# Seven half-size products in place of eight in the up projections of a fp32 MLP

## The chip, the cores and the metric

The kernel runs on one core of one Trainium2 chip. The metric is device time in microseconds of one execution, as the median of several. Its engines are called as the profile calls them: PE (matrix products), DVE (vectors), ACT (activations and copies), POOL (GpSimd), and SP, which here issues DMAs.

## The reference

The program is a block of two layers on 512 latent and 256 context tokens with D = 1024 and D_FF = 4096. Each layer runs four token mixers and then an MLP; what is changed is the MLP of layer 0, which works on all 768 tokens (layer 1 needs the latent ones only):

```python
def sq_relu_mlp(h, w1, b1, w2, b2):
    a = jax.nn.relu(h @ w1 + b1)
    return (a * a) @ w2 + b2
# in layer 0, for the latent stream and in the same way for the context
h2 = rmsnorm(x, ln2_g[l]) * (1.0 + sc2) + sh2
x = x + g2 * sq_relu_mlp(h2, mlp_w1[l], mlp_b1[l], mlp_w2[l], mlp_b2[l])
```

## The kernel before, in words

Activations lie with features on the 128 partitions and tokens along the row, latent tokens in 0 to 511, context tokens in 512 to 767. h2 is eight tiles k of 128 features, w1 has 32 columns f of 128, w2 has 32 k tiles and eight row tiles m.

Every fp32 product is made of three fp32r matmuls. An operand is split into a high part H (a cast) and a low part L (the rest), and H x bH, H x bL, L x bH are added in PSUM. `low` (L189) makes a split: the cast on ACT (L193), the subtraction through `tt` (L177) on POOL for weights and on DVE for activations. `load` (L309) brings a 256 KB weight block by one SP DMA (L315) into one of four `raw` buffers and splits it. `proj` (L323) runs the matmuls of one output tile through `mm` (L208, its matmul is L215): for weights (H, L) of four k tiles, first the 512 latent columns, then the 256 context columns.

`mlp` (L1740) works in eight chunks of four columns. `up(c)` makes four columns of h2 @ w1, each with 24 matmuls of 512 and 24 of 256 columns; `evac` applies bias and relu on ACT into `mr`, POOL squares into `mq`, and the split gives `y` and `aL`. `down(c)` runs, for each m, the four k tiles of the chunk against w2 and adds the result times g2 to x through `residual` (L1713), two DVE operations (L180) of 512 and 256 columns. The order is up(0), up(1), down(0), up(2), down(1) and so on:

```python
prev = None
for c in range(8):
    a = yield from up(c)
    if prev is not None:
        yield from down(c - 1, prev)
    prev = a
tail.append(down_last(prev))
```

The last down products, `down_last`, stand in `tail` and run inside the next layer's first stage, whose names begin with wa; at m = 1 and m = 6 it starts further work of the next layer (`near_end`). An accumulation of `down` takes one of two PSUM tiles of two banks (`p2`); there are two smaller ones as well (`p1`).

PE's order is written out by hand: `mm` chains each matmul behind the one before it, and a planner (`run`, `pipe`, `fill_step`) takes steps from the generators. At every seventh step of the MLP (`PACE["mlp"]`), and where a generator asks to wait, it fills in a step of other work, here the next layer's modulation (`mods`, tiles mod__m, lines L217 and L227); `drain` at the end of the layer runs what is left of it. The order on the other engines, SP's among them, is made by the language's scheduler.

## Time and profile before

| | us |
|---|---|
| median of 3 runs | 3298.92 (3297.35 to 3302.91) |
| the profiled execution | 3299.71 |
| its span in the trace | 3297.9 |
| PE busy | 3087.1 (94%) |
| DVE busy | 1391.9 (42%) |
| ACT busy | 1129.2 (34%) |
| POOL busy | 1373.4 (42%) |

The profile is of one execution. Busy shares are means over the whole program; a stage is read from windows of the trace. The up and down products of the changed MLP lie between about 1358 and 1878 us of the span, and its last down products behind that. A row's "idle before" names what ended the wait of that engine. "L215" is a line of the kernel before.

### The profile page before, as it was taken

How to read it: one execution, taken by the hardware profiler on the slowest of the kernel's cores; microseconds unless marked ns; L12 is line 12 of the kernel's file. 1: busy time of each engine (PE TensorE's matmuls, PEld its weight loads, DVE VectorE, ACT ScalarE, POOL GpSimd, SP SyncE). 2: the span in 40 equal slices, each digit the busy share in tenths (PEclk: the TensorE clock that was granted, in tenths of full speed). 3: DMA queues.
4: the chain of work that ended last, by engine and by line, in shares of the span. 5: the costliest groups of instructions: out<-in, count | busy, mean ns of one | idle time of the engine just before them, and what ended most of it. 6: DMA issues, size and time to landing. Idle time of an engine off the chain costs nothing. (4 is left out here: it accounts for less than half of the span.)

```text
span 3297.9 us, 48613 instructions
## 1 busy us (share of the span) xinstructions
PE 3087.1 (94%) x18344; PEld 2615.3 (79%) x18344; DVE 1391.9 (42%) x2920; ACT 1129.2 (34%) x2133; POOL 1373.4 (42%) x1126
## 2 busy tenths in 40 slices
PE   7888989899999999999999987889999999999999
PEld 5777778788888888888888876777877788788887
DVE  6644522554444454511221276444354444442223
ACT  5434423334332122422222254333333432243333
POOL 4422232323344453443333355224333455555553
PEclk9999999999999999999999988999999999999999
DMA  7343343333243456222222334444333343823332
GB/s 270 105 117 100 123 144 97 90 100 114 74 144 95 137 172 199 64 77 75 74 74 74 94 100 118 138 131 118 104 108 102 106 143 110 271 78 99 96 96 80
DMA packets 556922, 380.24 MB, mean 115 GB/s; under 512 B 45177, under 2 KB 503870, under 8 KB 556688
## 3 DMA queue, kind: packets, MB, share of 16 engines
q1 hardware_dynamic: 556056, 376.98, 38.0%
q8 instruction: 145, 2.38, 0.3%
q14 instruction: 89, 0.73, 0.1%
q10 hardware_dynamic: 632, 0.16, 0.0%
HBM read 307.52 MB, written 63.75 MB: 113 GB/s over the span
## 5 line engine op out<-in xcount | busy, mean ns | idle before, releaser
L177 POOL TENSOR_TENSOR mlp__wL<-mlp__raw,mlp__wH 128x512 fp32r<-128x512 f32 x268 | 351.6, 1314 | 455.0 <-ACT mlp__wH L193 321.4
L193 ACT CAST mlp__wH<-mlp__raw 128x512 fp32r<-128x512 f32 x268 | 166.1, 621 | 499.9 <-PE mlp__p L215 350.2
L177 POOL TENSOR_TENSOR gt__wL<-gt__raw,gt__wH 128x512 fp32r<-128x512 f32 x128 | 169.2, 1328 | 277.6 <-ACT gt__wH L193 231.2
L215 PE MATMUL mlp__p<-out__hL,mlp__wH 128*128 128x512 f32 (+1 forms) x760 | 257.1, 353 | 3.8 <-DVE out__hL L517 2.0
L215 PE MATMUL mlp__p<-out__hH,mlp__wH 128*128 128x512 f32 (+1 forms) x760 | 259.8, 353 | 0.5 <-ACT out__hH L516 0.5
L180 DVE SCALAR_TENSOR_TENSOR mlp__x<-mlp__p,modT,mlp__x 128x512 f32<-128x512 f32 (+1 forms) x169 | 106.4, 657 | 335.4 <-PE mlp__p L215 329.2
L215 PE MATMUL mlp__p<-mlp__y,mlp__wH 128*128 128x512 f32 (+1 forms) x672 | 231.9, 356 | 0.0
L215 PE MATMUL mlp__p<-mlp__aL,mlp__wH 128*128 128x512 f32 (+1 forms) x672 | 231.2, 355 | 0.0
L177 DVE TENSOR_TENSOR mlp__aL<-mlp__mq,mlp__y 128x768 fp32r<-128x768 f32 (+1 forms) x64 | 85.7, 1339 | 302.4 <-ACT mlp__y L193 302.2
L215 PE MATMUL gt__m<-mod__hH,gt__wH 128*128 128x512 f32 (+1 forms) x512 | 172.4, 353 | 8.1 <-DVE spec__filt L177 3.2
L215 PE MATMUL mlp__p<-out__hH,mlp__wL 128*128 128x512 f32 (+1 forms) x760 | 177.6, 351 | 0.0
L215 PE MATMUL gt__m<-mod__hL,gt__wH 128*128 128x512 f32 (+1 forms) x512 | 167.3, 343 | 0.0
L215 PEld LDWEIGHTS mlp__p<-out__hL,mlp__wH 128*128 128x128 f32 x760 | 143.5, 190 | 24.8 <-DVE out__hL L517 3.2
L177 POOL TENSOR_TENSOR ml__wL<-ml__raw,ml__wH 128x512 fp32r<-128x512 f32 x64 | 84.0, 1312 | 190.1 <-ACT ml__wH L193 171.8
L215 PEld LDWEIGHTS mlp__p<-out__hH,mlp__wH 128*128 128x128 f32 x760 | 144.3, 190 | 22.0 <-issue 2.2
L215 PE MATMUL mlp__p<-mlp__y,mlp__wL 128*128 128x512 f32 (+1 forms) x672 | 155.8, 354 | 0.0
L215 PEld LDWEIGHTS mlp__p<-out__hH,mlp__wL 128*128 128x128 f32 x760 | 130.3, 190 | 18.8
L215 PEld LDWEIGHTS mlp__p<-mlp__y,mlp__wH 128*128 128x128 f32 x672 | 126.8, 189 | 19.9 <-issue 2.2
L215 PEld LDWEIGHTS mlp__p<-mlp__aL,mlp__wH 128*128 128x128 f32 x672 | 127.1, 189 | 18.0
L193 ACT CAST gt__wH<-gt__raw 128x512 fp32r<-128x512 f32 x128 | 79.1, 619 | 177.4 <-DMA gt__raw<-in_w_in_dram 114.4
L215 PEld LDWEIGHTS mlp__p<-mlp__y,mlp__wL 128*128 128x128 f32 x672 | 115.0, 189 | 17.6
L215 PEld LDWEIGHTS gt__m<-mod__hH,gt__wH 128*128 128x128 f32 x512 | 98.5, 192 | 21.4 <-DVE spec__filt L177 5.2
(574 smaller groups left out, 7948.4 us busy)
## 6 DMA issues: line engine op xcount, KB each, us to landing
mlp__raw<-in_mlp_w_dram SPq DMA_DIRECT2D x240, 256.0 KB
mod__raw<-in_w_mod_dram SPq DMA_DIRECT2D x160, 256.0 KB
gt__raw<-in_w_in_dram SPq DMA_DIRECT2D x128, 256.0 KB
ml__raw<-in_w_in_dram SPq DMA_DIRECT2D x64, 256.0 KB
hy__raw<-in_w_in_dram SPq DMA_DIRECT2D x48, 256.0 KB
spec<-spec__kk SPq DMA_DIRECT2D x80, 128.0 KB
ga__raw<-in_w_in_dram SPq DMA_DIRECT2D x32, 256.0 KB
hy__spec<-spec SPq DMA_DIRECT2D x16, 512.0 KB
```

The source lines that it names most:

```text
L177: (eng or nc.vector).tensor_tensor(o, a, b, op)
L180: nc.vector.scalar_tensor_tensor(o, a, s, b, op0, op1)
L193: nc.scalar.copy(H, src)
L215: in_order(nc.tensor.matmul(ps, lhsT=a, rhs=b, start=start, stop=stop_), cost)
```

## The change

In layer 0 alone (`fast`) the MLP works in 16 chunks of two columns. Columns 0 to 3 are made as before. The other 28 go by pairs: `pair(f)` treats columns f and f + 1, times the two halves of the k tiles, as a 2 x 2 block matrix of weights, and h2, k halves by token halves of 384, as the other one, and forms their product by the seven-product scheme of Strassen in Winograd's order of additions. A product is 12 matmuls of 384 columns on four k tiles.

- `combos()` makes the sums of activation blocks once: for each of four k, the operations on DVE that are marked tr, ts, tt and t3, and three splits. It is a generator that stands in the pipe beside the MLP (`later`). `into_b12` splits the last of them into hH and hL in place.
- `pair` loads four blocks of w1, forms four combinations of weights on DVE (ws, w1r, raw, raw), and splits seven blocks, where the two columns had four. The products' results are put together by one ACT copy and seven DVE additions of 384 columns, six of them into `wu` and `mr`, and relu runs on those.
- The square is formed in place (`squared`).
- `weights2` loads two row tiles m of w2 in one block; `down` runs two k tiles for each m, 16 chunks of eight accumulations, with twice as many calls of `residual`.
- `mod_units(..., ahead=False)` changes the order of the modulation steps' loads.

The core of the diff (left out are the parts of `proj` that put `nk` for 4, and unchanged surroundings):

```diff
+
+        fast = len(segs) > 1
+        step = 2 if fast else 4
+        last_c = 32 // step - 1
+        half = w.stop // 2
+        lo_, hi_ = slice(0, half), slice(half, 2 * half)
+        T = {}
+        early = []
+
+        def combos():
+
+            while not all(p in hdone for p in pieces):
+                yield 0.3
+            whole = lambda k: (hH[:, k, w].bitcast(F32), hL[:, k, w].bitcast(F32))
+            homes = [yslot(), yslot(), yslot(), yslot(), big(F32R, "tc"), big(F32R, "tc"), big(F32R, "tc"), big(F32R, "tc")]
+            homes += [sp.tile([P, TOT], F32R, tag="g", name=uid("tc"), bufs=4) for _ in range(3)] + [slot(F32R, "tc")]
+            hold = [slot(name="t3") for _ in range(2)]
+            for k in range(4):
+                r, s, t = slot(name="tr"), slot(name="ts"), slot(name="tt")
+                tt(r[:, w], *whole(k), ALU.add)
+                tt(s[:, w], *whole(4 + k), ALU.add)
+                tt(t[:, lo_], r[:, hi_], r[:, lo_], ALU.subtract)
+                yield 1.5
+                tt(t[:, hi_], s[:, hi_], t[:, lo_], ALU.subtract)
+                T[3, k] = hold[k // 2][:, hi_ if k % 2 else lo_]
+                tt(T[3, k], s[:, hi_], r[:, hi_], ALU.subtract)
+                H, L = homes[2 * k], homes[2 * k + 1]
+                low(H[:, w], L[:, w], t[:, w])
+                T[1, k], T[2, k] = (H[:, lo_], L[:, lo_]), (H[:, hi_], L[:, hi_])
+                yield 1.5
+                tt(s[:, lo_], s[:, lo_], t[:, hi_], ALU.subtract)
+                H, L = (homes[8 + 2 * (k // 2) + x][:, hi_ if k % 2 else lo_] for x in range(2))
+                low(H, L, s[:, lo_])
+                T[4, k] = H, L
+                yield 4.0
+            T["all"] = True
+
+        def into_b12():
+
+            for k in range(4):
+                low(hH[:, k, hi_], hL[:, k, hi_], T[3, k])
+
+        def b(i, j):
+            return lambda k: (hH[:, 4 * i + k, hi_ if j else lo_], hL[:, 4 * i + k, hi_ if j else lo_])
+
+        def product(ps, W, mov_):
+            H, L = W
+            for k in range(4):
+                bH, bL = mov_(k)
+                mm(ps, H[:, k, :], bH, k == 0, False)
+                mm(ps, H[:, k, :], bL, False, False)
+            for k in range(4):
+                mm(ps, L[:, k, :], mov_(k)[0], False, k == 3)
+            yield 0.0
+
+        def pair(f):
+
+            while "all" not in T:
+                yield 0.3
+            if f == 4:
+                into_b12()
+            A = {}
+            view = lambda t: t.rearrange("p (k n) -> p k n", k=4)
+            for i, x in ((0, 0), (1, 0), (1, 1), (0, 1)):
+                A[i, x] = slot(name="w1r")[:, :512] if i else rawtile()
+                src = I["mlp_w1"][l][:, (f + i) * P : (f + i + 1) * P]
+                newest[0] = nc.sync.dma_start(view(A[i, x]), wcols(src, x).rearrange("(k p) n -> p k n", p=P))
+            s1 = slot(name="ws")[:, :512]
+
+            def split(t):
+                H, L = whalf()
+                low(H, L, view(t), leng=nc.gpsimd)
+                return H, L
+
+            W11 = split(A[0, 0])
+            tt(s1, A[1, 0], A[1, 1], ALU.add)
+            tt(A[1, 0], A[0, 0], A[1, 0], ALU.subtract)
+            tt(A[0, 0], s1, A[0, 0], ALU.subtract)
+            W2 = split(A[0, 0])
+            W12 = split(A[0, 1])
+            tt(A[0, 1], A[0, 1], A[0, 0], ALU.subtract)
+            W3 = split(A[1, 0])
+            pp_ = p2()
+            pa, pc_ = pp_[:, 0:half], pp_[:, 512 : 512 + half]
+            pb_, pd = p1()[:, :half], p1()[:, :half]
+            x_, u_, r0, r1 = (slot(name=n) for n in ("wx", "wu", "mr", "mr"))
+            bias = [vcol(vt, "mlp_b1", f + i) for i in range(2)]
+            relu = lambda d, s, i: act(d, s, AF.Relu, bias=bias[i])
+            yield from product(pa, W11, b(0, 0))
+            nc.scalar.copy(x_[:, lo_], pa)
+            W1 = split(s1)
+            yield from product(pb_, W2, lambda k: T[2, k])
+            tt(x_[:, hi_], pb_, x_[:, lo_], ALU.add)
+            W22 = split(A[1, 1])
+            yield from product(pc_, W12, b(1, 0))
+            tt(r0[:, lo_], pc_, x_[:, lo_], ALU.add)
+            relu(r0[:, lo_], r0[:, lo_], 0)
+            W4 = split(A[0, 1])
+            yield from product(pd, W3, b(0, 1))
+            tt(u_[:, lo_], pd, x_[:, hi_], ALU.add)
+            yield from product(pa, W1, lambda k: T[1, k])
+            tt(u_[:, hi_], pa, x_[:, hi_], ALU.add)
+            tt(r1[:, hi_], pa, u_[:, lo_], ALU.add)
+            yield from product(pb_, W22, lambda k: T[4, k])
+            tt(r1[:, lo_], pb_, u_[:, lo_], ALU.add)
+            relu(r1[:, w], r1[:, w], 1)
+            yield from product(pc_, W4, b(1, 1))
+            tt(r0[:, hi_], pc_, u_[:, hi_], ALU.add)
+            relu(r0[:, hi_], r0[:, hi_], 0)
+            return r1, r0
+
+        def squared(r, a):
+            tt(r[:, w], r[:, w], r[:, w], ALU.mult, eng=nc.gpsimd)
+            H, L = yslot(), big(F32R, "aL")
+            low(H[:, w], L[:, w], r[:, w])
+            a.append((H, L))
+
         def up(c):
-            a, early = [], []
-            for j in range(4):
-                f = c * 4 + j
-                if c == 0 and j < 3:
-                    if j == 0:
+            a = []
+            if fast and c >= 2:
+                for r in (yield from pair(2 * c)):
+                    squared(r, a)
+                return a[::-1]
+            for j in range(step):
...
-                r, q = slot(name="mr"), slot(name="mq")
+                r = slot(name="mr")
                 evac(r, ps, lambda d, a: act(d, a, AF.Relu, bias=vcol(vt, "mlp_b1", f)))
-                tt(q[:, w], r[:, w], r[:, w], ALU.mult, eng=nc.gpsimd)
-                H, L = yslot(), big(F32R, "aL")
-                low(H[:, w], L[:, w], q[:, w])
-                a.append((H, L))
+                squared(r, a)
             return a
 
-        def weights2(c, m):
-            return load(I["mlp_w2"][l][c * 512 : (c + 1) * 512, m * P : (m + 1) * P])
+        def weights2(c, m, kept=[None]):
+
+            if not fast:
+                return load(I["mlp_w2"][l][c * 512 : (c + 1) * 512, m * P : (m + 1) * P])
+            if m % 2 == 0:
+                src = I["mlp_w2"][l][c * 256 : (c + 1) * 256, m * P : (m + 2) * P].rearrange("(k p) (m n) -> p k m n", p=P, m=2)
+
+                def get(raw):
+                    newest[0] = nc.sync.dma_start(raw.rearrange("p (k m) n -> p k m n", m=2), src)
+                kept[0] = load(get)
+            return [t[:, m % 2 :: 2, :] for t in kept[0]]
 
         def down(c, a):
             for m in range(KD):
                 ps = acc_tile(segs)
                 W = weights2(c, m)
-                yield from proj(ps, [W], lambda k: a[k])
+                yield from proj(ps, [W], lambda k: a[k], step)
...
+        if fast:
+            strands.append(combos())
         prev = None
-        for c in range(8):
+        for c in range(last_c + 1):
             a = yield from up(c)
             if prev is not None:
                 yield from down(c - 1, prev)
...
-    def mod_units(l, js):
+    def mod_units(l, js, ahead=True):
         blocks = [mod_block(l, vts[l], j) for j in js]
+        if not ahead:
+            return [u for us, last_ in blocks for u in us + [last_]]
         us = list(blocks[0][0])
...
+
+    def later(gens):
+
+        def f():
+            while not gens:
+                yield 0.3
+            yield from gens[0]
+        return [f()] if len(segs) > 1 else []
 
...
         if l + 1 < DEPTH:
-            mods.extend(mod_units(l + 1, range(4)))
+            mods.extend(mod_units(l + 1, range(4), False))
...
-        body = mlp(l, vt, xs, hview(hH, hL), segs, next_layer, by_pieces(pieces, hdone), pieces, made, tail)
-        run(f"mlp{l}", pipe(before + [body], 9), pace=PACE["mlp"])
+        beside = []
+        body = mlp(l, vt, xs, hview(hH, hL), hH, hL, segs, next_layer, by_pieces(pieces, hdone), pieces, made, tail, beside)
+        run(f"mlp{l}", pipe(itertools.chain(before, [body], later(beside)), 9), pace=PACE["mlp"])
         drain()
```

Where instructions stand now. A number behind a name is that of a buffer.

DVE at the end of the first down products, `down(0)`; x are the residual's tiles, p a PSUM tile, aL the split of a column. Before:

```order
L180 SCALAR_TENSOR_TENSOR mlp__x_12507<-mlp__p_2548_13623,modT_106,mlp__x_12507 128x512
L180 SCALAR_TENSOR_TENSOR mlp__x_12507<-mlp__p_2548_13623,modT_106,mlp__x_12507 128x256
L180 SCALAR_TENSOR_TENSOR out__x_12524<-mlp__p_2552_13658,modT_106,out__x_12524 128x512
L180 SCALAR_TENSOR_TENSOR out__x_12524<-mlp__p_2552_13658,modT_106,out__x_12524 128x256
L177 TENSOR_TENSOR mlp__aL_13766<-mlp__mq_13762,mlp__y_13765 128x768
L177 TENSOR_TENSOR mlp__aL_13837<-mlp__mq_13833,mlp__y_13836 128x768
L177 TENSOR_TENSOR mlp__aL_13906<-mlp__mq_13902,mlp__y_13905 128x768
```

And now:

```order
L180 SCALAR_TENSOR_TENSOR mlp__x_12507<-mlp__p_2488_13245,modT_106,mlp__x_12507 128x512
L180 SCALAR_TENSOR_TENSOR mlp__x_12507<-mlp__p_2488_13245,modT_106,mlp__x_12507 128x256
L180 SCALAR_TENSOR_TENSOR out__x_12524<-mlp__p_2492_13268,modT_106,out__x_12524 128x512
L180 SCALAR_TENSOR_TENSOR out__x_12524<-mlp__p_2492_13268,modT_106,out__x_12524 128x256
L398 TENSOR_REDUCE mod__s_2495_13292<-mod__m_13287 128x8
L177 TENSOR_TENSOR modT_107<-mod__s_2495_13292,vec_489 128x8
L177 TENSOR_TENSOR mlp__tc_13306<-mlp__ts_13356,mlp__tc_13305 128x384
L177 TENSOR_TENSOR mlp__tr_13377<-out__hH_12097,out__hL_12098 128x768
L177 TENSOR_TENSOR mlp__ts_13378<-out__hH_12097,out__hL_12098 128x768
L177 TENSOR_TENSOR mlp__tt_13379<-mlp__tr_13377 128x384
L177 TENSOR_TENSOR mlp__t_2509_13308<-mlp__ts_13378,mlp__tr_13377 128x384
L177 TENSOR_TENSOR mlp__tt_13379<-mlp__ts_13378,mlp__tt_13379 128x384
```

Of the 27 operations of the first three k of `combos` and `into_b12`, 26 stand ahead of these, up to six from one residual to the next; the 27th (tc) and all nine of the fourth k stand behind the last residual, with the first pair's weights (ws, w1r, raw). Before, the splits of the next columns stood there.

DVE in a later `down`, the one that stands before the third pair (columns 8 and 9):

```order
L177 TENSOR_TENSOR mlp__w1r_14045<-mlp__raw_14043,mlp__w1r_14045 128x512
L180 SCALAR_TENSOR_TENSOR mlp__x_12100<-mlp__p_2619_13890,modT_106,mlp__x_12100 128x512
L180 SCALAR_TENSOR_TENSOR mlp__x_12100<-mlp__p_2619_13890,modT_106,mlp__x_12100 128x256
L177 TENSOR_TENSOR mlp__aL_13882<-mlp__mr_13766,mlp__y_13881 128x768
L177 TENSOR_TENSOR mlp__aL_13887<-mlp__mr_13765,mlp__y_13886 128x768
L180 SCALAR_TENSOR_TENSOR mlp__x_12165<-mlp__p_2624_13918,modT_106,mlp__x_12165 128x512
L180 SCALAR_TENSOR_TENSOR mlp__x_12165<-mlp__p_2624_13918,modT_106,mlp__x_12165 128x256
L177 TENSOR_TENSOR mlp__raw_14043<-mlp__ws_14051,mlp__raw_14043 128x512
L180 SCALAR_TENSOR_TENSOR mlp__x_12234<-mlp__p_2625_13933,modT_106,mlp__x_12234 128x512
L180 SCALAR_TENSOR_TENSOR mlp__x_12234<-mlp__p_2625_13933,modT_106,mlp__x_12234 128x256
L180 SCALAR_TENSOR_TENSOR mlp__x_12299<-mlp__p_2629_13954,modT_106,mlp__x_12299 128x512
```

Two splits aL, and a weight combination in front of them and behind the second residual, stand between residuals; before, the residual pairs of a `down` followed one another, with one split among them all.

PE at the end of `mlp`, before:

```order
L215 MATMUL mlp__p_3042_17051<-mlp__y_16089,mlp__wL_17055 128x256
L215 MATMUL mlp__p_3042_17051<-mlp__y_16163,mlp__wL_17055 128x256
L215 MATMUL mlp__p_3042_17051<-mlp__y_16232,mlp__wL_17055 128x256
L217 MATMUL mod__m_17086<-mod__raw_17009,scp 32x128 x4
L217 MATMUL mod__m_17086<-mod__raw_17084,scp 32x128 x4
L217 MATMUL mod__m_17100<-mod__raw_17091,scp 32x128 x4
L217 MATMUL mod__m_17100<-mod__raw_17098,scp 32x128 x4
L227 MATMUL mod__m_17110<-ident,mod__g_15032 128x128 x4
L227 MATMUL mod__m_17118<-ident,mod__g_16516 128x128 x4
L215 MATMUL wa__p_3061_17141<-mlp__y_16588,wa__wH_17137 128x512
L215 MATMUL wa__p_3061_17141<-mlp__aL_16589,wa__wH_17137 128x512
```

And now:

```order
L215 MATMUL mlp__p_3264_17703<-mlp__y_17268,mlp__wH_17685 128x256
L215 MATMUL mlp__p_3264_17703<-mlp__aL_17269,mlp__wH_17685 128x256
L215 MATMUL mlp__p_3264_17703<-mlp__y_17273,mlp__wL_17686 128x256
L215 MATMUL mlp__p_3264_17703<-mlp__y_17268,mlp__wL_17686 128x256
L215 MATMUL wa__p_3271_17733<-mlp__y_17570,wa__wH_17729 128x512
L215 MATMUL wa__p_3271_17733<-mlp__aL_17571,wa__wH_17729 128x512
L215 MATMUL wa__p_3271_17733<-mlp__y_17565,wa__wH_17729 128x512
L215 MATMUL wa__p_3271_17733<-mlp__aL_17566,wa__wH_17729 128x512
```

The modulation matmuls (mod__m) that stood between the MLP's products and the last down products (wa__p) are no longer there. On SP, where three of their loads and three of constants stood ahead of the first weights of the last down products (wa__raw), those now follow the MLP's own directly.

## Rows read from the trace of the kernel before

**Rows 1.** the profile's page: its head and busy time by engine

```profile
span 3297.9 us, 48613 instructions
...
PE 3087.1 (94%) x18344; PEld 2615.3 (79%) x18344; DVE 1391.9 (42%) x2920; ACT 1129.2 (34%) x2133; POOL 1373.4 (42%) x1126
```

**Rows 2.** windows: stretch, length, PE, PEld, DVE, ACT, POOL busy, PEclk, DMA, GB/s

```profile
1395.00:1545.00 150.00, 150.00 (x896) 129.99 (x896) 28.82 (x41) 38.57 (x59) 61.60 (x47) 1.00 0.27 78
1545.00:1683.00 138.00, 138.00 (x826) 119.64 (x825) 27.01 (x42) 33.78 (x52) 52.98 (x40) 1.00 0.26 74
...
1878.00:1922.00 44.00, 38.28 (x204) 31.68 (x204) 22.53 (x41) 18.25 (x33) 17.21 (x13) 0.96 0.48 140
```

**Rows 3.** PE timeline, 1545 to 1553: start, length, instruction, idle before and releaser

```profile
1545.64 0.40 PE L215 MATMUL mlp__p<-out__hH,mlp__wH 128*128 128x512 f32 x1
...
1548.39 0.28 PE L215 MATMUL mlp__p<-out__hH,mlp__wH 128*128 128x256 f32 x1
...
1549.82 0.40 PE L215 MATMUL mlp__p<-out__hH,mlp__wH 128*128 128x512 f32 x1
...
1552.66 0.43 PE L217 MATMUL mod__m<-mod__raw,scp 128*32 128x128 f32 x8
```

**Rows 4.** timelines of PE and SP where the MLP ends

```profile
1883.69 0.80 PE L215 MATMUL wa__p<-mlp__y,wa__wH 128*128 128x512 f32 x1 [4.71 <-ACT wa__wH L193]
...
1886.80 0.39 PE L215 MATMUL wa__p<-mlp__aL,wa__wH 128*128 128x512 f32 x1
...
1877.35 0.92 SPq L315 DMA_DIRECT2D wa__raw<-in_mlp_w_dram  x2
```

**Rows 5.** groups by shape, 1545 to 1683: busy us, mean ns, idle

```profile
L177 POOL TENSOR_TENSOR mlp__wL<-mlp__raw,mlp__wH 128x512 fp32r<-128x512 f32 x32 | 41.6, 1300 | 78.7 <-ACT mlp__wH L193 78.7
L177 POOL TENSOR_TENSOR mlp__mq<-mlp__mr 128x768 f32<-128x768 f32 x8 | 11.7, 1468 | 5.8 <-ACT mlp__mr L184 5.8
...
L193 ACT CAST mlp__wH<-mlp__raw 128x512 fp32r<-128x512 f32 x32 | 19.8, 620 | 81.6 <-DMA mlp__raw<-in_mlp_w_dram 42.0 <-PE mlp__p L215 39.5
...
L180 DVE SCALAR_TENSOR_TENSOR mlp__x<-mlp__p,modT,mlp__x 128x512 f32<-128x512 f32 x14 | 10.5, 751 | 51.6 <-PE mlp__p L215 51.6
L177 DVE TENSOR_TENSOR mlp__aL<-mlp__mq,mlp__y 128x768 fp32r<-128x768 f32 x8 | 8.5, 1066 | 41.9 <-ACT mlp__y L193 41.9
```

**Rows 6.** timelines of DVE and PE, 1545 to 1572

```profile
1545.55 0.96 DVE L177 TENSOR_TENSOR mlp__aL<-mlp__mq,mlp__y 128x768 fp32r<-128x768 f32 x1 [11.67 <-ACT mlp__y L193]
...
1571.48 1.14 DVE L180 SCALAR_TENSOR_TENSOR mlp__x<-mlp__p,modT,mlp__x 128x512 f32<-128x512 f32 x2 [7.65 <-PE mlp__p L215]
...
1571.28 0.40 PE L215 MATMUL mlp__p<-mlp__y,mlp__wH 128*128 128x512 f32 x1
```

**Rows 7.** DVE's groups over the whole span, by shape

```profile
L177 DVE TENSOR_TENSOR hy__c<-hy__p,hy__spec 128x256 f32<-128x256 f32 x160 | 56.3, 418 | 57.7 <-PE hy__p L215 57.7
...
L177 DVE TENSOR_TENSOR spec__kk<-spec__ev,spec__m 128x512 f32<-128x512 f32 x32 | 20.6, 683 | 8.1 <-PE spec__m L215 6.4 <-DMA spec<-spec__kk 1.8
...
L177 DVE TENSOR_TENSOR ml__mW<-ml__mW,ml__kq 128x384 f32<-128x384 f32 x16 | 8.8, 547 | 0.3 <-ACT ml__mW L184 0.3
...
L177 DVE TENSOR_TENSOR ga__gr<-ga__gsq,ga__gsw 128x512 f32<-128x512 f32 x12 | 8.3, 688 | 0.6
```

**Rows 8.** timelines of DVE and PE at the MLP's start, 1393 to 1396

```profile
1393.13 1.17 DVE L177 TENSOR_TENSOR mlp__aL<-mlp__mq,mlp__y 128x768 fp32r<-128x768 f32 x1 [2.23 <-ACT mlp__y L193]
...
1395.42 0.40 PE L215 MATMUL mlp__p<-out__hH,mlp__wH 128*128 128x512 f32 x1
```

**Rows 9.** timelines of DVE and POOL, 3068 to 3071 and 1386 to 1391

```profile
3069.42 1.37 DVE L177 TENSOR_TENSOR mlp__aL<-mlp__mq,mlp__y 128x512 fp32r<-128x512 f32 x1
...
3068.95 1.29 POOL L177 TENSOR_TENSOR mlp__wL<-mlp__raw,mlp__wH 128x512 fp32r<-128x512 f32 x1 [0.43 <-PE mlp__p L215]
...
1386.86 4.04 DVE L177 TENSOR_TENSOR mlp__aL<-mlp__mq,mlp__y 128x768 fp32r<-128x768 f32 x2 [7.26 <-ACT mlp__y L193]
...
1388.06 2.02 POOL L177 TENSOR_TENSOR mlp__wL<-mlp__raw,mlp__wH 128x512 fp32r<-128x512 f32 x1
```

25 lines of the change are left out of this document (14 added, 11 removed).

## The prediction

> **What bounds the kernel now.** I read the page first, then busy time by stage, then PE's and DVE's timelines in the MLP of layer 0, then the grouped instructions that supply prices, and last the place where that MLP ends. The page shows PE busy 94% of the span and DVE 42% [rows 1]. By stage it is sharper: over 1395 to 1545 and 1545 to 1683 PE is busy for the whole stretch at a granted clock of 1.00 (2.4 GHz), while DVE has 28.82 of 150 and 27.01 of 138 us and POOL 61.60 and 52.98 [rows 2]. So here every matmul column removed is time won, as long as DVE and POOL, which get the new work, stay out of PE's way. The stretch behind it, 1878 to 1922, has PE idle for 5.72 us, and that is where the old MLP hands over to its last down products [rows 2].
>
> **What is removed on PE.** Twelve 512-column matmuls take 1548.39 - 1545.64 = 2.75 us, twelve 256-column ones 1549.82 - 1548.39 = 1.43 [rows 3], so 229 and 119 ns each. A column of w1 has 24 of either: 8.36 us, a pair 16.72. No row shows a 384-column matmul of this kind; its price lies between 119 and 229 ns, and since the two known ones are linear within a few ns I take the middle, 174. A product of the new scheme is 12 of them, 2.09 us; seven are 14.63. That saves 2.09 us per pair and over 14 pairs **29.3 us**. The ends: at 119 ns 94 us saved, at 229 ns 35 lost; both need the price of another width, so I keep 2.5 ns on either side, which over 14 x 84 matmuls is 3 us: 26 to 32. The Trainium skill, "TensorE: Matmul & The Clock Gate", section "Back-to-back issue gap", gives an isolated gap of N/2.4 + 2.5 ns; by it a 384-column matmul would be 162.5 ns, a product 1.95 us and the saving 27.3. It also gives 216 ns at 512 columns where the rows show 229, so the rows stand.
>
> The down products keep their columns. Their 64 accumulations become 128 of half the depth: six matmuls of each width, 1.38 + 0.72 = 2.09 us, where there were 4.18.
>
> **The handover: -6.2 us.** Before, SP issues the weights of the last down products only at 1877.35, behind the left-over modulation work, and PE stands 4.71 us for them; after that wait its first seven 512-column matmuls take 1886.80 - 1883.69 = 3.11 us [rows 4] where seven take 1.60 at the pace of [rows 3], the 1.2 GHz level for most of it, 1.5 us. In the changed order no modulation work is left at the handover and these loads follow the MLP's own on SP. The wait goes, and the slow start with it: 4.7 + 1.5 = 6.2. Ends: 6.2 and, if the weights are still late by one split (0.62 + 1.30, [rows 5]), 4.
>
> **The start: +18 us.** All 14 pairs stand behind the combinations of the activations. For each of four k they are three DVE operations of 768 columns and six of 384 (the last into hL). The 768-column split takes 0.96 undisturbed [rows 6] and a 384-column operation with both operands in SBUF 0.547 [rows 7]: 4 x (2.88 + 3.28) = 24.6 us. In the same stretch stand the eight residual pairs of the first down products at 1.14 [rows 6], 9.1; the split of column 3, 1.0; and three of the first pair's weight operations at 0.69 [rows 7], 2.1, the last of which gives product 2 its weights. Together 36.8 us, from when DVE has its third split done, 1393.13 + 1.17 = 1394.3 [rows 8]: 1431.1, and with the cast and POOL's subtraction behind it, 0.62 + 1.30 [rows 5], 1433.0. PE without a wait would come to product 2 at 1395.4 [rows 8] + 8 x 2.09 + 2.09 = 1414.2. It is 18.8 us late; six modulation steps of 0.43 [rows 3] fall into the gap, -2.6; and DVE loses some 2 to POOL (below). That is +18. Bounds: the fourth k's nine operations and the weights stand wholly behind the last residual in the order, so even if all else hides, 1.3 + 8.3 + 1.9 less product 1's 2.1 and the modulation steps is 7; at the other end each 768-column operation takes the mean 1.066 or more and the rest is blocked too, 22. PE restarts at the lower clock: +1.5, as at the handover [rows 4].
>
> **The steady cycles: +12 us.** A cycle is now seven products and eight down accumulations, 14.63 + 16.72 = 31.35 us of PE. In the seven products DVE has seven additions with a PSUM operand, 384 columns, between 418 and 683 ns [rows 7], say 551: 3.9 of 14.6, hidden. In the eight accumulations it has 9.1 of residuals, three weight operations, 2.1, and two activation splits, 1.9: 13.1 of 16.7, hidden on average. POOL has 11 splits and 2 squares [rows 5], 17.2 of 31.3. What decides is the order. Two accumulators alternate. A residual starts 0.20 us after its product ends (1571.28 to 1571.48) and takes 1.14 [rows 6], so one other operation of 0.96 before the next residual fits: 1.34 + 0.96 = 2.30 against 2.09 + 0.20. Two just fit: 1.34 + 0.96 + 0.69 + 1.14 puts the next residual's end at 4.13, and PE wants that buffer at 4.18. They cost nothing alone, but an operation that meets a POOL split waits it out: one of 128x512 took 1.37 while a POOL split ran, where 0.69 is usual [rows 7, 9]. One such meeting, 1.30, stalls PE by 4.13 + 1.30 - 4.18 = 1.25. In the order, nine down stretches (those that prepare pairs 6 to 22) have two SBUF operations between residuals somewhere, and the four that prepare pairs 24 to 30 alternate. I take one meeting in each of the nine: 9 x 1.3 = **11.7**. Ends: 2 (no meeting, only late weights now and then) and 28 (two in each of the nine, 23.4, and twice in each of the four a single operation that meets one, 0.56 each, 4.5).
>
> **The tail: +2 us.** The last down products cover 16.7 us of the next stage's vector work in place of 33.4, with two residual pairs where one was. Nothing in the trace prices that; 0 and one more wait like the 4.71 bound it.
>
> **Sum**: -29.3 - 6.2 + 18 + 1.5 + 11.7 + 2 = -2.3. The profiled execution took 3299.71 (span 3297.9), so 3297.4; the median of the runs is 0.8 lower, which gives **3297 us**. What a measurement here can tell from no change is 0.2%, 6.6 us: by this sum the change gives back nearly all it wins.
>
> **Rivals.**
> *DVE stays hidden after all.* For it: DVE's 42% [rows 1], and 13.1 of 16.7. Against it: the start, where one chain stands before the products. Then start 7, slow restart 1.5, cycles 2, no tail: -25.0, 3274; with up to six meetings in the cycles 3282.
> *The order is as slow as the locks allow* (the slower side). DVE's two-SBUF-operand operations and POOL's splits shut one another out: 1.37 for 0.69, and 4.04 for two 0.96 splits beside a POOL split that took 2.02 [rows 9]. The Trainium skill, "SBUF — State Buffer", section "Who interferes with whom", has the same as a rule: a DVE operation with two SBUF inputs and a GpSimd one that reads SBUF lock each other out fully; the trace agrees. The change multiplies both kinds. If DVE meets two splits between residuals in each of the nine cycles, the accumulators become the bound: start 22, cycles 28, tail 2: -35.5 + 22 + 1.5 + 28 + 2 = +18, 3317; it decides from some 3.6 us of blocking in a cycle (16.7 - 13.1). Against it: the residuals read PSUM, and their mean of 0.751 at 512 columns [rows 5] shows no blocking.
> *The change doesn't do what it says*: a 384-column matmul priced like one of 512 would make products of 2.75 us and lose 35. Against it: 256 columns cost 119, nearly in proportion [rows 3].
>
> **How the numbers follow.** Forecast 0.50 (own range 3288 to 3304), DVE hidden 0.25, locks 0.22, width 0.03. Faster by over 0.2%, below 3292.3: the second case and a quarter of the first, 0.38. Slower, above 3305.5: four fifths of the third, the fourth, and a few of the first: 0.25. Same: 0.37. The range reaches to 3279, which leaves out the better half of the second case, and to 3314, which leaves out the worse part of the third and the fourth.
>
> **What would show it.** Right: PE gaps of about 20 us in all at the first pair's second product, ended by DVE through a weight split; no 4.71 wait at the handover; 12 x 384 columns in 2.09 us; short PE waits on residuals in the nine down stretches, few after; DVE's 768 and 512 operations longer on average than 0.96 and 0.69. Wrong: a start gap below 10 us, or cycles of 31.4 us throughout (then the second case); cycles of over 34 us (the third); 384 columns far from 2.09 us per twelve.

## The result and the profile after

| | before | changed |
|---|---|---|
| median of 4 runs, us | 3300.82 (3297.35 to 3302.91) | 3328.13 (3321.77 to 3331.64) |
| ratio | | 1.0085, 95% interval 1.0068 to 1.0103 |
| profiled execution, us | 3299.71 | 3321.77 |

The change costs 27 us. The forecast was 3297, with a range up to 3314: it was wrong, and on the side of the second rival, the locks. The profiled execution is the shortest of the four and is 22.1 us over that of before; the account below is made between these two.

The page's head, and the windows of three of the same stretches as in [rows 1, 2] (the first from 1445, behind the start):

```profile
span 3320.0 us, 48802 instructions
...
PE 3074.8 (93%) x18176; PEld 2621.0 (79%) x18176; DVE 1588.1 (48%) x3238; ACT 1171.5 (35%) x2215; POOL 1442.4 (43%) x1168
...
1445.00:1545.00 100.00, 95.62 (x566) 86.00 (x565) 56.03 (x87) 32.24 (x54) 54.69 (x41) 1.00 0.28 81
1545.00:1683.00 138.00, 129.88 (x772) 115.61 (x771) 78.64 (x118) 41.73 (x69) 66.90 (x51) 0.99 0.26 78
1878.00:1922.00 44.00, 44.00 (x251) 39.60 (x250) 22.35 (x38) 14.14 (x23) 20.95 (x17) 1.00 0.37 111
```

PE is busy 12 us less in the whole than in [rows 1], and the span is 22 us longer. In the two middle windows PE has lost its full share (95.62 of 100, 129.88 of 138, where [rows 2] had all of it), and DVE has 56.03 of 100 and 78.64 of 138 us of work where it had 28.82 of 150 and 27.01 of 138. The place of the handover is clean: 44.00 of 44.

PE's rows for three terms of the sum, a product of 384 columns, the handover and the start:

```profile
1717.81 0.34 PE L215 MATMUL mlp__p<-out__hH,mlp__wH 128*128 128x384 f32 x1
...
1719.89 0.85 PE L215 MATMUL mlp__p<-mlp__y,mlp__wH 128*128 128x384 f32 x4
...
1916.07 0.40 PE L215 MATMUL mlp__p<-mlp__y,mlp__wL 128*128 128x256 f32 x2
1916.31 0.40 PE L215 MATMUL wa__p<-mlp__y,wa__wH 128*128 128x512 f32 x1
...
1431.93 0.69 PE L215 MATMUL mlp__p<-out__hH,mlp__wH 128*128 128x384 f32 x1 [3.72 <-ACT mlp__wH L193]
...
1437.37 0.96 PE L215 MATMUL mlp__p<-mlp__y,mlp__wH 128*128 128x384 f32 x4 [1.22 <-ACT mlp__wH L193]
```

A product is 1719.89 - 1717.81 = 2.08 us (2.09 forecast), the wait of 4.71 at the last down products is gone [rows 4], and the second product of the first pair starts at 1437.4. From 1431.93 to 1437.37, behind a wait of 3.72, the granted clock was 0.58, so PE ran mostly at 1.2 GHz there. What ended that wait, on SP, ACT and DVE:

```profile
1400.19 25.88 SPq L409 DMA_DIRECT2D mod__raw<-in_w_mod_dram  x7
1427.61 0.37 SPq L1817 DMA_DIRECT2D mlp__raw<-in_mlp_w_dram  x1
...
1431.26 0.62 ACT L193 CAST mlp__wH<-mlp__raw 128x512 fp32r<-128x512 f32 x1 [2.30 <-DMA mlp__raw<-in_mlp_w_dram]
...
1432.64 1.46 DVE L177 TENSOR_TENSOR mlp__tc<-mlp__tt,mlp__tc 128x768 fp32r<-128x768 f32 x1 [2.90 <-ACT mlp__tc L193]
```

SP issues the first load of the first pair's weights only at 1427.61, behind seven loads for modulation steps. ACT's cast waits 2.30 for it, PE waits for the cast, and DVE, with the last sums still to split, stands 2.90 for a cast that is queued on ACT behind that one.

Cycle by cycle PE's timeline gives the length of each stretch of seven products and of each `down` (16.72 is PE's own time in a `down`; a modulation step of eight matmuls is counted at 0.58, since a stretch of products with one lasts 15.15 and one without 14.57, a step of four at 0.43):

| | products | down | of it modulation steps, about | lost, about |
|---|---|---|---|---|
| start: first down and first pair | 18.65 | 34.48 | 5.7 | 16 |
| the nine down stretches with two operations between residuals | 15.0 to 15.2 | 18.9 to 22.4, sum 183.7 | 6.5 | 27 |
| the next four | 14.57 | 17.8, 17.8, 17.8, 17.9 | 0 | 4.5 |
| the last | 14.57 | 16.79 | 0 | 0 |

So the steady cycles lose some 31 us, where the forecast had 11.7. (What the products of the nine cycles have over 14.57 is modulation steps too.) A small part of it is the clock: behind the two longest waits of the nine, 2.46 and 2.81 us, the granted clock was 0.92 from 1660.54 to 1682.10 and 0.86 from 1743.22 to 1755.36, so PE ran some of that time at 1.2 GHz; by these shares, an estimate, that is 1.7 us each. PE's groups from 1360 to 1915, with their shapes apart, put the idle time in front of the first matmul of the down accumulations; the columns are busy time, mean and idle time before them with what ended it:

```profile
L215 PE MATMUL mlp__p<-mlp__y,mlp__wH 128*128 128x512 f32 x240 | 98.6, 411 | 27.6 <-DVE mlp__x L180 17.8 <-DVE mlp__mr L177 9.3 <-ACT mlp__wH L193 0.2
```

The residuals (L180) ended 17.8 us of it and the pairs' additions into mr (L177) 9.3. Matmul ends are modelled, so the lengths of the stretches count more than these sums; what they tell is who is waited for. This is what a loss looks like in one of the four that were called alternating, on PE and DVE (of PE the start of the stretch and of its second accumulation):

```profile
1769.93 0.39 PE L215 MATMUL mlp__p<-mlp__y,mlp__wH 128*128 128x512 f32 x1
...
1772.92 0.50 PE L215 MATMUL mlp__p<-mlp__y,mlp__wH 128*128 128x512 f32 x1 [0.74 <-DVE mlp__mr L177]
...
1770.52 1.15 DVE L177 TENSOR_TENSOR mlp__ws<-mlp__w1r,mlp__w1r 128x512 f32<-128x512 f32 x1 [1.92 <-DMA mlp__w1r<-in_mlp_w_dram]
1771.70 0.69 DVE L177 TENSOR_TENSOR mlp__w1r<-mlp__raw,mlp__w1r 128x512 f32<-128x512 f32 x1
1772.31 0.55 DVE L177 TENSOR_TENSOR mlp__mr<-mlp__p,mlp__wu 128x384 f32<-128x384 f32 x1
1772.78 0.68 DVE L177 TENSOR_TENSOR mlp__raw<-mlp__ws,mlp__raw 128x512 f32<-128x512 f32 x1
1773.38 1.14 DVE L180 SCALAR_TENSOR_TENSOR mlp__x<-mlp__p,modT,mlp__x 128x512 f32<-128x512 f32 x2
```

The pair's last addition, into mr, is free to run at about 1770.13, 0.2 us behind its product. It runs at 1772.31, because two sums of the next pair's weights stand in front of it on DVE: ws, which waited 1.92 us, at the end of it for its load, and then took 1.15 where 0.68 is usual, and w1r. That addition reads one half of an accumulator, so PE waits 0.74 for it at its second accumulation, and the first residual comes at 1773.38 in place of 1772.2.

### The profile page after: what moved, and what is told of

Read it like the earlier page. It is cut to its first block, busy times and chain, and to the rows that moved or that the text cites. A ratio compares the mean times of both kernels' runs of the same rounds, so it can differ in the third digit from the quotient of the medians.

```text
span 3320.0 us, 48802 instructions
## 1 busy us (share of the span) xinstructions
PE 3074.8 (93%) x18176; PEld 2621.0 (79%) x18176; DVE 1588.1 (48%) x3238; ACT 1171.5 (35%) x2215; POOL 1442.4 (43%) x1168
## 3 DMA queue, kind: packets, MB, share of 16 engines
q1 hardware_dynamic: 539672, 376.98, 37.6%
## 5 line engine op out<-in xcount | busy, mean ns | idle before, releaser
L177 POOL TENSOR_TENSOR mlp__wL<-mlp__raw,mlp__wH 128x512 fp32r<-128x512 f32 x272 | 365.8, 1348 | 344.8 <-ACT mlp__wH L193 200.5
L177 POOL TENSOR_TENSOR gt__wL<-gt__raw,gt__wH 128x512 fp32r<-128x512 f32 x128 | 169.9, 1333 | 306.9 <-ACT gt__wH L193 244.3
L215 PE MATMUL mlp__p<-mlp__y,mlp__wH 128*128 128x512 f32 (+2 forms) x816 | 273.5, 358 | 28.8 <-DVE mlp__x L180 17.8
L180 DVE SCALAR_TENSOR_TENSOR mlp__x<-mlp__p,modT,mlp__x 128x512 f32<-128x512 f32 (+1 forms) x281 | 169.2, 636 | 201.7 <-PE mlp__p L215 195.3
L215 PE MATMUL mlp__p<-mlp__aL,mlp__wH 128*128 128x512 f32 x704 | 245.8, 356 | 0.0
L215 PE MATMUL mlp__p<-mlp__y,mlp__wL 128*128 128x512 f32 x760 | 197.8, 354 | 0.0
L215 PE MATMUL mlp__p<-out__hH,mlp__wH 128*128 128x512 f32 (+2 forms) x536 | 192.0, 361 | 4.2 <-ACT mlp__wH L193 3.7
L215 PE MATMUL mlp__p<-out__hL,mlp__wH 128*128 128x512 f32 (+2 forms) x536 | 189.2, 360 | 3.3 <-DVE out__hL L517 2.2
L177 POOL TENSOR_TENSOR ml__wL<-ml__raw,ml__wH 128x512 fp32r<-128x512 f32 x64 | 85.6, 1338 | 178.3 <-ACT ml__wH L193 159.1
L177 DVE TENSOR_TENSOR mlp__aL<-mlp__mr,mlp__y 128x768 fp32r<-128x768 f32 (+1 forms) x64 | 89.7, 1402 | 131.8 <-ACT mlp__y L193 131.6
L215 PEld LDWEIGHTS mlp__p<-mlp__y,mlp__wL 128*128 128x128 f32 x760 | 135.2, 190 | 19.4
L215 PE MATMUL mlp__p<-out__hH,mlp__wL 128*128 128x512 f32 (+2 forms) x536 | 130.6, 358 | 0.0
L215 PEld LDWEIGHTS mlp__p<-out__hL,mlp__wH 128*128 128x128 f32 x536 | 101.6, 191 | 14.9 <-DVE out__hL L517 3.0
L215 PE MATMUL gt__m<-mod__hH,gt__wL 128*128 128x512 f32 (+1 forms) x512 | 112.0, 342 | 0.0
```

The source lines that it names most:

```text
L177: (eng or nc.vector).tensor_tensor(o, a, b, op)
L180: nc.vector.scalar_tensor_tensor(o, a, s, b, op0, op1)
L215: in_order(nc.tensor.matmul(ps, lhsT=a, rhs=b, start=start, stop=stop_), cost)
```

## The experiments

The versions below were compared with the kernel before on the same chip. "MLP" is the time from the first up product of layer 0 to the first of its last down products, read from PE's timeline in the one profiled execution of each; where the last four columns go together there, and for the kernel before, 16.7 us are added, so that the same work is counted.

| version | median us | ratio to before, interval | MLP us |
|---|---|---|---|
| before | 3300.23 to 3302.27 | | 542.3 |
| the change | 3328.13 | 1.0085 (1.0068 to 1.0103) | 556.2 |
| down by two alone | 3326.21 | 1.0083 (1.0066 to 1.0101) | 555.4 |
| the same, splits held | 3312.10 | 1.0025 (1.0014 to 1.0035) | 545.1 |
| weight sums late | 3303.29 | 1.0011 (0.9997 to 1.0025) | 535.4 |
| no activation sums | 3315.41, one run | | 547.1 |
| no weight sums | 3306.77, one run | | 535.3 |
| splits late at 4 and 5 | 3311.61 | 1.0030 (1.0017 to 1.0043) | 546.9 |
| last four together | 3295.74 | 0.9987 (0.9975 to 0.9999) | 534.9 |
| activation sums first | 3306.54 | 1.0012 (1.0000 to 1.0024) | 537.4 |
| before, next layer later | 3296.38 | 0.9977 (0.9967 to 0.9987) | 539.9 |
| one between | 3292.59 | 0.9971 (0.9959 to 0.9982) | 534.1 |
| planned start | 3277.97 | 0.9925 (0.9909 to 0.9941) | 520.0 |

**Down by two alone.** The change without pairs:

```diff
-            if fast and c >= 2:
+            if False:
...
-            strands.append(combos())
+            strands.append(iter(()))
```

> The down products by two k tiles as in the change, but all up columns made by full products as before: no activation sums, no weight sums, no half-size products. Theory (the steady loss comes from the sums on DVE and their waits, not from the halved accumulations): PE keeps its pace through the down stretches, the handover gains its 6.2 us, so the layer-0 MLP from its first down product to the last down products is about 6 us shorter than before apart from the moved 16.7 us, and the total is 3293 to 3301. Rival (twice the residual pairs and two alternating accumulators of half the depth stall PE by themselves): the down stretches last 18.5 us and more instead of 16.7, and the total is 3315 or more. If layer 1 still runs 5 to 9 us longer than before, that part of the loss belongs to the shorter last down stretch and the moved modulation, not to the half-size products.

Measured 3326.21: the theory as it stood fell. Without one half-size product the down stretches still last 16.8 to 22.2 us, and the MLP loses about 18 in all (555.4 - 542.3, and the 4.7 of the handover's wait, which is gone here too). This version keeps the change's loads of two row tiles of w2 in one block; what these do alone was not tried. ACT, DVE and PE in one of the worst:

```profile
1474.94 0.62 ACT L193 CAST mlp__wH<-mlp__raw 128x512 fp32r<-128x512 f32 x1 [3.45 <-DMA mlp__raw<-in_mlp_w_dram]
1475.47 0.83 ACT L193 CAST mlp__y<-mlp__mr 128x768 fp32r<-128x768 f32 x1
...
1476.33 1.46 DVE L177 TENSOR_TENSOR mlp__aL<-mlp__mr,mlp__y 128x768 fp32r<-128x768 f32 x1 [3.28 <-ACT mlp__y L193]
1477.71 2.18 DVE L180 SCALAR_TENSOR_TENSOR mlp__x<-mlp__p,modT,mlp__x 128x512 f32<-128x512 f32 x4
...
1478.90 0.50 PE L215 MATMUL mlp__p<-mlp__y,mlp__wH 128*128 128x512 f32 x1 [2.28 <-DVE mlp__x L180]
```

On ACT the cast of y stands behind a weight cast that waited 3.45 us for its load. On DVE the split aL needs that y, and the residuals of two accumulations queue behind it (x4 in one row). PE waits 2.28. Before, with accumulations of 4.18 us, PE stood nowhere in the windows of [rows 2].

**The same, splits held.** The subtraction of each split is emitted behind the residual of m = 2 or 4:

```diff
+                if m in SPLITS and pend:
+                    after(pend.pop(0)(), behind[m])
```

> Down products by two k tiles with all up columns by full products, as in the first experiment, but the two columns' activation splits on DVE held behind the residuals of m = 2 and 4. Theory (the halved accumulations cost nothing by themselves; it is a split that waits for its cast, in front of the residual of m = 1 or 2, that stops PE): the stretches of 18 to 22 us fall to 16.8 to 17.3 and the layer-0 MLP by 14 to 18 us, total 3306 to 3312, the rest being layer 1's loss. Rival (PE is stopped by twice the residuals as such): the total stays at 3320 or more.

3312.10, at the edge of what was expected; the MLP is 10.3 us shorter, not 14 to 18. So the waiting split is a little more than half of the 18 us. In what is left, two waits of 1.2 and 1.5 end on ACT's relu of a column, which holds the other accumulator; the rest is short and was not traced to one cause.

**Weight sums late.** In the change, the next pair's first three weight sums behind the residuals of m = 1, 2 and 3:

```diff
-            tt(s1, A[1, 0], A[1, 1], ALU.add)
+            after(nc.vector.tensor_tensor(s1, A[1, 0], A[1, 1], ALU.add), behind.get(1))
...
```

(and the next two in the same way)

> The change, with the next pair's first three weight sums held on DVE behind the residuals of m = 1, 2 and 3, so that none stands ahead of the last addition of a pair or of the first residual. Theory (a weight sum waits for its DMA and for POOL, and the last addition and the residuals queue behind it): the PE wait of 0.7 to 2.5 us at the second down product, ended by that addition, goes from all 13 cycles, the down stretches fall from 17.8 to 22.4 us to at most 18.5, and the total falls by 12 to 25 us from the change's 3328, to 3303 to 3316. Rival (it is the lock between DVE's and POOL's operations, whatever the order): the waits move to later residuals, the down stretches stay at 18 to 22 us on average 20, total 3320 to 3330.

3303.29, 25 us under the change, just at the better end. Its nine down stretches last 17.2 to 21.9 us, and the five behind them 16.8 without a wait. The MLP is 20.8 us shorter; the rest of the 25 lies outside it. One of the five on DVE:

```profile
1786.61 0.56 DVE L177 TENSOR_TENSOR mlp__mr<-mlp__p,mlp__wu 128x384 f32<-128x384 f32 x1 [1.52 <-PE mlp__p L215]
1788.70 1.14 DVE L180 SCALAR_TENSOR_TENSOR mlp__x<-mlp__p,modT,mlp__x 128x512 f32<-128x512 f32 x2 [1.54 <-PE mlp__p L215]
1789.76 0.95 DVE L177 TENSOR_TENSOR mlp__aL<-mlp__mr,mlp__y 128x768 fp32r<-128x768 f32 x1
1790.80 1.14 DVE L180 SCALAR_TENSOR_TENSOR mlp__x<-mlp__p,modT,mlp__x 128x512 f32<-128x512 f32 x2
1791.86 0.68 DVE L1829 TENSOR_TENSOR mlp__ws<-mlp__w1r,mlp__w1r 128x512 f32<-128x512 f32 x1
1792.46 0.95 DVE L177 TENSOR_TENSOR mlp__aL<-mlp__mr,mlp__y 128x768 fp32r<-128x768 f32 x1
1793.33 1.14 DVE L180 SCALAR_TENSOR_TENSOR mlp__x<-mlp__p,modT,mlp__x 128x512 f32<-128x512 f32 x2
```

The last addition follows its product, the first residual starts at 1788.70 and not 3.4 us into the stretch, and even two operations between residuals (ws 0.68, aL 0.95) fit, as the forecast's arithmetic had it, as long as neither waits.

Whether it was the waits or the locks between DVE and POOL that went, DVE's groups from 1437 to 1916 tell (mean and idle time before them); the first two lines are the change, the third this version:

```profile
L177 DVE TENSOR_TENSOR mlp__ws<-mlp__w1r,mlp__w1r 128x512 f32<-128x512 f32 x13 | 13.8, 1065 | 19.7 <-DMA mlp__w1r<-in_mlp_w_dram 19.6
L177 DVE TENSOR_TENSOR mlp__w1r<-mlp__raw,mlp__w1r 128x512 f32<-128x512 f32 x13 | 12.5, 965 | 6.6 <-DMA mlp__raw<-in_mlp_w_dram 6.4
...
L1829 DVE TENSOR_TENSOR mlp__ws<-mlp__w1r,mlp__w1r 128x512 f32<-128x512 f32 x14 | 10.1, 720 | 0.0
```

In the change ws and w1r stood 26 us for their loads; here neither waits at all. All weight sums together took 50.0 us there (53 operations) and 49.5 here (56), since the fourth, raw, which is not held, went from 1065 to 1444 ns on average; the splits aL fell from 37.1 to 32.4. By 0.68 and 0.95 undisturbed these operations lost 25 us to POOL in the change and 17 here, an estimate. So most of the locks are still there, at other places, and the waits for loads are gone. The longest stretch left, 21.9, has another wait: two splits aL that stand 2.93 for the cast of y, in front of a residual for which PE waits 2.77.

**No weight sums** (the blocks are split as loaded, so the products are of other blocks) and **no activation sums** (the products read plain blocks of h2):

```diff
-            tt(s1, A[1, 0], A[1, 1], ALU.add)
-            tt(A[1, 0], A[0, 0], A[1, 0], ALU.subtract)
-            tt(A[0, 0], s1, A[0, 0], ALU.subtract)
-            tt(A[0, 1], A[0, 1], A[0, 0], ALU.subtract)
```

> The change without the four sums of weight blocks per pair: the blocks are split as they are loaded, so the values differ; loads, the seven splits, activation sums, products and residuals are as in the change. Theory (the weight sums' waits on DMA and on POOL, in front of the last addition and between residuals, make most of the 33 us of the steady cycles): the down stretches of the 13 cycles fall to 17 to 17.5 us, total 25 us under the change, 3293 to 3303. Rival (the residuals and activation splits collide with POOL's splits anyway): the stretches stay at 19 us and more, total 3312 or more.

> The change without the sums of activations: the products read blocks of the activations as they are, so the values differ; weights, products, additions and residuals are as in the change. Theory (the start costs some 18 to 20 us because the DVE chain of 24 us stands before the second product): the first down stretch falls from 34.5 us to about 18 to 19 and the first pair starts without a gap, total some 18 us under the change's run with the profile (3322), 3300 to 3308. Rival (the start's gap comes from the first pair's weights): the gap before the second product stays over 8 us, and the total falls by less than 10.

Without weight sums the MLP takes 535.3, the same as with the sums held late: as far as the MLP shows it, all that they cost was their place. Without activation sums the first down stretch is 20.29 and the first pair 15.27 us, together 17.6 less than in the change, 3.5 of it modulation steps that stand in later stretches instead. The first pair's loads come earlier too (two at 1395.89), so the run does not tell the sums from these loads. And the MLP is only 9.1 us shorter (547.1), since the later down stretches reach 22.7 us. So the one total, 3315.41, which is 7 over what was expected, is a miss that the trace bears out. That without weight sums, 3306.77, is 4 over, within the scatter of single executions (the kernel before ran between 3290 and 3310 in 27 runs).

**Splits late at 4 and 5.** Weight sums late, and the two splits behind the residuals of m = 4 and 5; the fourth weight sum was left to the scheduler:

> The version with the weight sums held behind the residuals of m = 1 to 3, and also the two activation splits of a pair (the DVE subtraction alone) held behind the residuals of m = 4 and 5. Theory (with accumulations of half the depth any DVE operation that waits, for a DMA or for a cast, in front of a residual stops PE, because the slack to the next use of the accumulator is 0.65 us): the waits of 0.3 to 2.8 us that end on a residual go, the nine down stretches with modulation fall from 18.4 us on average to at most 17.5, and the total falls from 3303 by 6 to 11 us, to 3292 to 3297. Rival (the remaining excess is the modulation steps and the locks with POOL): no more than 3 us, 3300 to 3304.

3311.61, worse by 8. In the last five cycles the stretches became 18.1, since the next product waited 1.16, and in the eight before them it waited 0.5 to 1.9: the scheduler put the fourth sum right behind the second split. DVE, and POOL at the same time:

```profile
1810.90 0.99 DVE L1867 TENSOR_TENSOR mlp__aL<-mlp__mr,mlp__y 128x768 fp32r<-128x768 f32 x1
1811.82 1.78 DVE L177 TENSOR_TENSOR mlp__raw<-mlp__raw,mlp__raw 128x512 f32<-128x512 f32 x1
1813.52 1.13 DVE L180 SCALAR_TENSOR_TENSOR mlp__x<-mlp__p,modT,mlp__x 128x512 f32<-128x512 f32 x2
...
1811.04 2.01 POOL L177 TENSOR_TENSOR mlp__wL<-mlp__w1r,mlp__wH 128x512 fp32r<-128x512 f32 x1
```

aL and raw together, 0.99 and 1.78 (0.68 undisturbed), with a POOL split running: one operation that meets a split, behind another one, costs PE 1.16 here, where the forecast's price was 1.25. That price was near.

**Last four together.** With the weight sums late, the last two pairs' down products are not split in two chunks but run as four k tiles in the next layer's first stage:

```diff
...
-            if prev is not None:
+            if prev is not None and (c < last_c or not fast):
                 yield from down(c - 1, prev)
+            elif prev is not None:
+                a = prev + a
```

> The version with the weight sums held late, and the last two pairs' down products run together, four k tiles to an accumulation, as the last down products in the next layer's first stage, so that these take 33.4 us again in place of 16.7. Theory (the 7 to 12 us that layer 1 loses in every version so far come from the shorter cover for its first stage's norm and filters): layer 1's loss from the last down products to the end falls by 5 to 8 us, total 3295 to 3298. Rival (the loss comes from the modulation steps drained early or from the order of their loads): it stays, 3301 to 3305.

3295.74: as expected in size, but the theory is not shown by it. In the profiled execution, the slowest of the ten (3303.12), the time from the last down products to the end is 1404.3 us, 16.7 taken off, where the version with late sums has 1405.0; and these products now wait 4.4 us for the last pair's y.

**Before, next layer later.**

```diff
-                if m in (1, 6):
-                    near_end(m == 6)
+                if m in (4, 7):
+                    near_end(m == 7)
```

> The kernel before, with the two steps of the last down products that start the next layer's filters and modulation moved from m = 1 and 6 to m = 4 and 7, so that as much PE work lies behind them as in the change (some 16 and 4 us). Theory (layer 1 loses because that work starts later against the end of the last down products): total 5 to 9 us over before, 3305 to 3309. Rival (it is the moved modulation, the loads' order or the residuals): no difference above 2 us.

0.2% under before, so the start of the filters is not what layer 1 loses by. In its trace the wait at the handover is 2.34 in place of 4.71. SP issues these weights no earlier (1881.00, in a trace whose MLP starts 3.6 us later, against 1877.35 [rows 4]), and three loads of constants stand ahead of them in both, though not the same three. Why they land sooner is not shown.

**Activation sums first.** On the version with late weight sums:

```diff
-        run(f"mlp{l}", pipe(itertools.chain(before, [body], later(beside)), 9), pace=PACE["mlp"])
+        run(f"mlp{l}", pipe(itertools.chain(before, later(beside), [body]), 9), pace=PACE["mlp"])
```

> The version with the weight sums held late, and the generator of the activation sums placed ahead of the MLP's in the planner, so that they stand on DVE behind the norm, from 1382 us on, beside columns 2 and 3 and the first down products, and not only beside the first down products. Theory (the start's loss is one DVE chain that begins too late): the first down stretch falls from 35.8 us to 18 to 24, the gap before the second product to under 4 us, and the total falls by 8 to 16 us, to 3287 to 3295. Rival (the chain only moves the wait: splits and residuals behind it come later by as much): total 3300 or more.

No gain. The first down stretch and the first pair fall by 12 us together, but the sums now stand between the last operations of the norm, for which PE waits (1.15 and 2.50 on hL); columns 0 to 3 take 42.7 us in place of 37.3. The modulation steps, which had filled the gap, went into later down stretches.

**One between.** Last four together, with a DVE order of at most one operation between residuals (weight sums behind m = 1, 2, 3, 5, splits behind 4 and 6):

> The version with the last two pairs' down products together, and in every down stretch from the first pair on a DVE order with at most one other operation between two residuals: weight sums behind m = 1, 2, 3 and 5, activation splits behind m = 4 and 6. Theory (a second operation, or one that waits, between two residuals stops PE, one that is ready does not): the ten later down stretches last 16.8 us plus 0.4 per modulation step, where holding two at one place gave 18.1 and a wait of 1.16 at the next product; total 3 to 8 us under the version with the last four, some 3288 to 3293. Rival (POOL's locks stop DVE whatever the order): the stretches stay above 17.5 us and the total does not fall.

3292.59, inside the expectation. In the last five cycles the stretches are 17.4, not 16.8: PE lost 0.6 a cycle, most of it in a wait of 0.43 on a weight cast before the next product.

**Planned start.** The pairs begin at column 6, and the activation sums are emitted one by one, each held behind an operation:

```diff
-            if fast and c >= 2:
+            if fast and c >= 3:
...
+        def some(n, at):
+            for x in itertools.islice(work, n):
+                after(x, at)
...
+                if fast and c < 2:
+                    some(GAPS[c].get(m, 0), behind[m])
```

> The version before this one, with columns 4 and 5 made by full products too (13 pairs in place of 14, 2.1 us of the saving given up), so that the activation sums have the stretch from 1387 to 1447 us, and with their DVE operations placed by hand: eight beside column 3, one behind a residual in the first down products, 18 beside columns 4 and 5, the last four in the second down products. Theory (the start's 18 us are a DVE chain before the first pair that has no other work beside it): the gap before the first pair's second product falls to under 2 us, the first down stretch to 17 to 19, the total by 10 to 16 us, to 3276 to 3284, a ratio of 0.991 to 0.995. Rival (the 25 us of sums cost PE the same wherever they stand): total 3288 or more.

3277.97, a ratio of 0.9925 (0.9909 to 0.9941): faster than the kernel before and than the change. The start of its first down products on DVE, and PE at the first pair:

```profile
1406.99 1.14 DVE L180 SCALAR_TENSOR_TENSOR mlp__x<-mlp__p,modT,mlp__x 128x512 f32<-128x512 f32 x2
1408.05 0.99 DVE L1772 TENSOR_TENSOR mlp__tr<-out__hH,out__hL 128x768 f32<-128x768 f32 x1
1409.81 1.14 DVE L180 SCALAR_TENSOR_TENSOR mlp__x<-mlp__p,modT,mlp__x 128x512 f32<-128x512 f32 x2 [0.77 <-PE mlp__p L215]
1410.87 0.95 DVE L1773 TENSOR_TENSOR mlp__ts<-out__hH,out__hL 128x768 f32<-128x768 f32 x1
1411.91 1.14 DVE L180 SCALAR_TENSOR_TENSOR mlp__x<-mlp__p,modT,mlp__x 128x512 f32<-128x512 f32 x2
...
1459.82 0.41 PE L215 MATMUL mlp__p<-out__hH,mlp__wH 128*128 128x384 f32 x1 [0.29 <-DVE mlp__x L180]
...
1461.98 0.33 PE L215 MATMUL mlp__p<-mlp__y,mlp__wH 128*128 128x384 f32 x1
```

Between two residual pairs stands one sum. The first product waits 0.29, the second follows in 2.16, and the first two down stretches are 19.4 and 19.3 us, where the first alone took 34.5. The sums and the operations are all still there.

## Why the prediction was wrong

- **Products: right.** 14.57 us for seven where 14.63 was forecast; 30.1 us over 14 pairs. The Trainium skill, "TensorE: Matmul & The Clock Gate", section "Back-to-back issue gap", would make a product 1.95 us, an estimate from its isolated gap; the trace, with 2.08, does not agree.
- **Handover: right.** No wait there, and the granted clock is 1.00 from 1878 to 1922.
- **The start: near in size, its path right in part.** 19.5 was forecast, 1.5 of it for the slower restart; some 16 was measured. The chain of sums was the main cause: with the sums placed by hand beside other work, and the pairs begun a column pair later, all but about 3 us of it goes. But the forecast had one gap, at the second product, ended by DVE. The trace has four waits of 1.5 to 1.8 on residuals, between which sums stand, 3.72 before the first product and 1.22 before the second; and the 3.72 is for weights whose load was issued late, which is no term of the forecast. What these loads cost apart from the sums was not tried.
- **The steady cycles failed.** The step read "I take one meeting in each of the nine: 9 x 1.3 = 11.7", and the four others were called clean. They lost some 27 and 4.5, and from one pair to the next the nine took 33.9 to 37.6 us with their modulation steps (the first, behind the slow start, apart), where the prediction's own sign for the locks was over 34. The price of a meeting was near, 1.16 against 1.25; what was wrong is that every operation was taken to be ready when its turn came, so that only its length counted. In the traces DVE runs its operations in the order in which they stand: the sums of the next pair, which stand ahead of the last addition (ws and w1r in front of r0's), wait 26 us in all for their loads, and the splits wait for a cast on ACT that itself queues behind a load (3.4 in the change, more in "down by two alone"). Behind them wait the residuals, and behind those PE, since halving the accumulation left it 0.75 us of room (2.09 - 0.20 - 1.14). Holding the sums late took 25 us off the change, 20.8 of it in the MLP, with all DVE work and all POOL splits left in and 17 of the 25 us lost to POOL still lost, so it is the place, not the locks as such, that cost most. The locks are in the rows (1.78 for 0.68); they and the waiting splits are what is left, and how the last 10 us or so divide between them is not shown. The Trainium skill, "SBUF — State Buffer", section "Who interferes with whom", has them as a rule for which of two operations blocks the other; the rows agree (1.78 for 0.68 beside a POOL split), but the rule speaks only of one operation and the one that it meets, not of what is queued behind.
- **The halved accumulations were priced only as DVE work.** Alone, without a half-size product, they make the MLP as long as the whole change does (555.4 and 556.2 us), with splits that wait for casts. The change's 30 us of saved products pay for the start and a part of the steady cycles; that its losses are this version's and the sums' waits added up is not shown.
- **The rival that came nearest** (3317, by the locks) had the direction and, with 28 for the cycles, nearly their price; that was luck, since the cause was mostly another, as the experiment with late sums shows.
- **The tail: right as far as it can be told.** From the last down products to layer 1's next stage the change loses 2.9 us against before, where 2 was forecast and the restart's 1.5 is won back in the same stretch. From there on it loses another 3.3, which cannot be told from chance: there the kernel before, "one between" and "planned start" have one and the same order on PE, and took 1053.1, 1059.7 and 1054.8 us. The same holds for the 2.0 us by which the changed kernel's first up product came late, in code that the change leaves alone. Together: 2.0 - 30.1 - 4.7 + 16 + 31 + 2.9 + 3.3 = 20.4, of the 22.1 between the two profiled executions.

## What to carry to other kernels

When work is moved to an engine that has time on average, write down for each of its operations what it waits for, not only how long it runs: DVE ran its operations in the order in which they stood, so one early operation that waits for a load holds up everything behind it, and here that was worth 25 us with no work removed. Halving an accumulation halves the room for such delays, so check what stands between an accumulator's last matmul and its release. And a long preparing chain was nearly free here once it was spread, one operation to a gap, over work that does not depend on it; look as well at which loads its emission puts ahead of the next weights.
